# A hybrid decoder layer on one core: row maxima 0.75 of a head ahead of the attention instead of 0.65, and the maxima given during a wait for a shift counted

## The chip, the core and the metric

The kernel runs on one core of one Trainium2 chip. The metric is device time in microseconds (us) of one execution, lower is better. The core has a matrix engine (TensorE, called PE), a vector engine (DVE), a scalar engine (ACT), a general engine (POOL), and a queue engine (SP) that issues most transfers; each runs its own list of instructions in order and waits on the others through semaphores.

## What is computed

One layer of a decoder: a prompt of 2048 positions with model width 1024, and eight sampled positions with a paged cache (the sampled part is not touched by the change). RMSNorm and one input projection give q, k, v of 8 heads of 64, a forget gate, and the features za, u, gv, zc. One half is attention with a forget term, the other a spatial gating inside chunks of 128; both are gated and go through one output projection.

```python
def fox_prompt(q, k, v, logf):            # c is the running sum of logf
    ...
        s = jnp.einsum('bqhd,bkhd->bhqk', qb, kf) * SCALE
        s = s + cb[:, :, :, None] - c[:, :, None, :]
        s = jnp.where(pos_k[None, :] <= pos_q[:, None], s, -jnp.inf)
        pr = jax.nn.softmax(s, axis=-1)
        return jnp.einsum('bhqk,bkhd->bqhd', pr, vf)
...
def merge(x, attn, za, mix, u, zc, w_out):
    a = attn.astype(x.dtype).reshape(B, S, D_ATT) * jax.nn.silu(za)
    m = (u * mix.astype(x.dtype)).reshape(B, S, D_CHK) * jax.nn.silu(zc)
    return x + jnp.concatenate([a, m], axis=-1) @ w_out
```

## The kernel before

PE's program order is written out by hand; the other engines' instructions are issued by the same code as it goes along, and each engine runs them in that order. A clock in the code (`Pe.clock`, a sum of nominal costs of what has been put on PE) says when loads and late pieces of work are issued. The program has three stretches: the input products (to about 585 us), the attention loop (585 to about 1140 us), and the output products.

**The attention loop** goes over 32 units (head h, block c of 512 queries) in the order of the list `UNITS`. A unit has 4c+4 key tiles of 128 keys. For each key tile `values` puts on PE a pair of matmuls into a PSUM bank `sc` (three banks), on diagonal tiles with a small mask matmul between them; ACT takes the exponential into a tile `p` (line 1059, ten slots in turn); POOL adds `p` into the denominator `acc` (lines 1066 and 1068), and PE multiplies the `p` tiles with the values in batches of eight (`av`).

**The maxima.** Softmax needs a shift per query. It is the row maximum of the scores, computed ahead by a generator, `all_maxima` (its object is `mgen`), that runs head by head: matmuls of up to 512 columns into three PSUM banks `tp` (in the trace `tp<-k,q`), each followed by a DVE reduction of the bank (`mn<-tp`, lines 993 and 995). When four query tiles, one block c, are done, `shifts` has the result transposed on PE, copied by ACT (`rows<-tp`, line 1014) and stored by SP (`mrow<-rows`, line 1017), and puts (h, c) in the set `shifted`. A head has 17408 columns of maxima and the whole attention 8 heads of them. The first maximum of head h needs the head's key tile `k`, whose last three rows come from `kx` by a transfer on SP's queue (line 909). `load_head(h + 1)` queues these loads when unit (h, 0) reaches its second key tile, and they are issued one at a time as `Pe.clock` goes on.

**The rate of the maxima.** `mdone[0]` is the work of maxima given so far, `vdone` that of the key tiles; `MT` and `VT` are one head's share of each. In front of the first unit maxima are given until `mdone[0]` reaches `AHEAD * MT`. After each key tile the loop gives maxima as long as

```python
            while mdone[0] / MT < min(vdone / VT + AHEAD, NH):
```

**Waiting for a shift.** Four key tiles before a unit's end (or earlier) `values` calls `load_queries` for the next unit, which issues four transfers on SP's queue (lines 953 to 955; the last is the shift, from `mrow`). If the unit's shift isn't in `shifted`, `load_queries` takes maxima from the generator until it is (or calls `give`, which takes other filling products, when no maxima are left).

**Filling products** between key tiles are feature products (`fl<-hh,fh` and the like, three matmuls of 512 columns each time) and at the end output products.

**The end of the loop.** `load_out_weights` loads eight blocks of the output weights (`raw`, three buffers, line 1137); each is cast on ACT (`wo<-raw`, line 268) and subtracted on DVE (line 273) in the same queues that hold the exponentials and the reductions. `out_inputs` loads two tiles of 512 KB, `g` and `xy`, for each output row tile (lines 1171 and 1172), and casts `g` on ACT into `am`.

Of the kernel before, what the change touches and what calls it, by code (L numbers as in the profile page):

```python
# [56 lines left out]
NTP = 3  # L57
NAV = 1
UNITS = [(h, c) for h in range(6) for c in range(4)] + [(6, 0), (6, 1), (6, 2), (7, 0), (6, 3), (7, 1), (7, 2), (7, 3)]
AHEAD = 0.65  # L60
LSTEP = 3000.0
LHEAD = 2500.0
VPARTS = 7
# [23 lines left out]
def hymba_step(ctx, tc, x_prompt, x_sample, cache_k, cache_v, cache_logf, page_table, g_norm, w_in,  # L87
# [84 lines left out]
    def give():  # L172

        seen, last = len(nc.cur_bb.bb.instructions), Pe.last
        Pe.waiting.pop(0)[2]()
        for i in nc.cur_bb.bb.instructions[seen:] if last is not None else ():
            if i.engine != mybir.EngineType.PE:
                tc.add_manual_dep(i, last.name, mybir.DependencyInfo(mybir.DependencyClass.NoSync,
                                                                     mybir.DependencyReason.DATA), reason="given late")

    def pump(all_=False):
        while Pe.waiting and (all_ or Pe.waiting[0][0] <= Pe.clock):
            give()
        if not all_ and Pe.loads and Pe.clock >= Pe.load_at:
            load_next()
        if not all_ and Pe.clock >= Pe.side:
            m = next(mgen)
            mdone[0] += m
            Pe.side = Pe.clock + PACE if mdone[0] < AHEAD * MT else 1e12
        if not all_ and Pe.clock >= Pe.decode:  # L190
            Pe.decode = Pe.clock + (next(Pe.steps, None) or 1e12)

    def load_next():
        Pe.loads.pop(0)()
        Pe.load_at = Pe.clock + LSTEP
# [738 lines left out]
    def place(t):  # L934

        at = places.setdefault(t, [])
        if len(at) < 2:
            at.append(s4(F32R, t))
            nc.gpsimd.memset(at[-1][HD:HD + 3, 512 if t == "q2" else 0:].bitcast(F32), 1.0)
        else:  # L940
            at.append(at.pop(0))
        return at[-1]

    def load_queries(h, c):
        while (h, c) not in shifted:
            if next(mgen, None) is None:
                give()
            pump()

        t = place("q2")  # L950
        a, cs = h * HD, slice(c * 512, (c + 1) * 512)
        for r in range(2):
            nc.sync.dma_start(t[r * HD:(r + 1) * HD, :512].bitcast(F32), qk_hi[a:a + HD, cs])
        nc.sync.dma_start(t[:HD, 512:].bitcast(F32), qk_lo[a:a + HD, cs])
        nc.sync.dma_start(t[HD + 2:HD + 3, 512:].bitcast(F32), mrow[h:h + 1, cs])
        return t
# [79 lines left out]
    def values(at):  # L1036
# [3 lines left out]
        for kt in range(4 * c + 4):  # L1040
# [3 lines left out]
            if at + 1 < len(UNITS) and UNITS[at + 1] not in qload and kt >= 4 * c + 4 - (  # L1044
                    QLEAD if UNITS[at + 1] in shifted else 4):
                qload[UNITS[at + 1]] = load_queries(*UNITS[at + 1])
# [69 lines left out]
    def all_maxima():  # L1116
        for h in range(NH):
            while h not in heads or "k2" not in heads[h] or h and len(Pe.loads) > VPARTS:
                if not Pe.loads:
                    raise RuntimeError(h)  # L1120
                load_next()
            yield from maxima(heads[h])
# [109 lines left out]
    mgen = all_maxima()  # L1232
    mdone = [0.0]
# [113 lines left out]
    Pe.side = 1e12  # L1347
    while mdone[0] < AHEAD * MT:
        c = next(mgen)
        mdone[0] += c  # L1350
        fill(c * PRE)
        pump()
        if UNITS[0] in shifted and UNITS[0] not in qload:
            qload[UNITS[0]] = load_queries(*UNITS[0])
    if UNITS[0] not in qload:
        qload[UNITS[0]] = load_queries(*UNITS[0])
    vdone = 0.0
    for at, (h, c) in enumerate(UNITS):
# [5 lines left out]
        for v in values(at):  # L1364
            vdone += v
            fill(v * dose)
            pump()
            while mdone[0] / MT < min(vdone / VT + AHEAD, NH):
                m = next(mgen, None)
# [49 lines left out]
```

## Time and profile before

| what | value |
|---|---|
| runs | 1324.32, 1329.95, 1331.84 us; median 1329.95 us |
| profiled execution | 1327.27 us, of it 1325.5 us from its first to its last instruction (the span) |
| PE busy in the span | 1294.4 us (98%) |
| DVE, ACT, POOL busy | 49%, 33%, 42% |
| mean granted clock of PE | 0.990 of full speed |

All stretches that follow are in us from the span's start, in this one profiled execution. "Busy" of PE counts a matmul at half clock as longer, so a busy PE may still be a slow one. Start to start is the better measure of a matmul, as neighbours overlap.

### The profile page before, as it was taken

What the parts mean: (1) busy time and instruction counts of PE and PEld (TensorE: products, weight loads), DVE (VectorE), ACT (ScalarE), POOL (GpSimd) and SP (SyncE); (2) the same over time, 40 slices, a digit from 0 to 9 for tenths busy, and PEclk for the clock granted to TensorE, in tenths of its full rate; (3) what the DMA queues carried; (4) which work ended last, traced back from release to release, by engine and by line L of the source; (5) the groups of instructions that cost most, each with busy time, mean ns of one, the idle gap of its engine ahead of it and who ended that gap; (6) DMA issues with size and microseconds to landing.
All of it is one profiled execution on the core that took longest, in us unless ns stands there. A gap on an engine that the chain in (4) does not pass through costs nothing.

```text
span 1325.5 us, 19295 instructions
## 1 busy us (share of the span) xinstructions
PE 1294.4 (98%) x6544; PEld 1005.0 (76%) x6544; DVE 653.7 (49%) x1217; ACT 432.0 (33%) x781; POOL 559.9 (42%) x587
## 2 busy tenths in 40 slices
PE   6999999999999999999999999999999998999998
PEld 6999999999887877866666666666666564688877
DVE  5446664534678654254476544454455544422321
ACT  5542322222222111124444544344444356200100
POOL 3113343423232456215667565567567468600000
PEclk9999999999999999999999999999999898999999
DMA  7644353555213878946344856766474445573221
GB/s 218 197 122 106 88 144 112 151 144 149 73 43 83 291 240 261 310 112 157 81 129 132 221 137 164 205 175 174 131 204 118 112 131 173 184 265 118 96 81 48
DMA packets 189172, 201.43 MB, mean 152 GB/s; under 512 B 40018, under 2 KB 138642, under 8 KB 189050
## 3 DMA queue, kind: packets, MB, share of 16 engines
q1 hardware_dynamic: 185186, 191.43, 50.4%
q10 hardware_dynamic: 3488, 8.39, 1.7%
q8 instruction: 52, 0.85, 0.3%
q14 instruction: 46, 0.38, 0.1%
q0 software_dynamic: 400, 0.38, 0.1%
HBM read 127.43 MB, written 72.73 MB: 151 GB/s over the span
## 4 chain that ended last, share of the span: by engine, by line
PE 89%; DVE 3%; DMA 3%; issue 2%; ACT 1%; POOL 1%; SPq 1%; POOLq 0%; DVEq 0%; ACTq 0%
PE acc L198 35%; PE sc L198 23%; PE fl L198 10%; PE av L198 9%; PE tp L198 6%; PE tp L202 4%; PE pm L198 3%; POOL acc L1068 1%; DMA raw<-in_w_out_dram 1%; DVE mn L995 1%; DMA xp<-in_x_prompt_dram 0%; DMA wraw<-in_w_in_dram 0%; DVE mn L993 0%; DVE wl L281 0%; ACT p L1059 0%
## 5 line engine op out<-in xcount | busy, mean ns | idle before, releaser
L1068 POOL TENSOR_TENSOR acc<-acc,p 128x512 f32<-128x512 f32 (+3 forms) x256 | 289.4, 1131 | 78.7 <-ACT p L1059 63.1
L1059 ACT ACTIVATE p<-sc,zero 128x512 f32<-128x512 f32 (+1 forms) x320 | 194.0, 625 | 171.0 <-PE sc L198 162.6
L198 PE MATMUL acc<-wh,hh 128*128 128x384 f32 (+2 forms) x640 | 228.7, 357 | 0.8 <-ACT hh L268 0.8
L198 PE MATMUL acc<-wl,hh 128*128 128x384 f32 (+2 forms) x640 | 222.5, 348 | 1.0 <-DVE wl L281 1.0
L198 PE MATMUL acc<-wh,hl 128*128 128x384 f32 (+2 forms) x640 | 222.8, 348 | 0.7 <-DVE hl L273 0.6
L198 PE MATMUL sc<-q,k 128*128 128x512 f32 (+7 forms) x640 | 202.7, 398 | 6.7 <-ACT p L1059 6.6
L198 PE MATMUL sc<-wo,am 128*128 128x512 f32 x720 | 164.1, 390 | 0.0
L198 PEld LDWEIGHTS sc<-wo,am 128*128 128x128 f32 x720 | 134.9, 188 | 28.2
L995 DVE TENSOR_REDUCE mn<-tp 128x1 f32<-128x320 f32 (+5 forms) x192 | 118.9, 632 | 75.5 <-PE tp L198 74.6
L198 PEld LDWEIGHTS sc<-q,k 128*128 128x128 f32 (+1 forms) x640 | 119.1, 197 | 27.1 <-ACT p L1059 11.4
L198 PE MATMUL av<-p,vst 128*64 128x512 f32 (+3 forms) x640 | 137.2, 549 | 0.0
L198 PE MATMUL tp<-k,q 66*128 66x384 f32 (+6 forms) x320 | 122.3, 399 | 8.5 <-DMA k<-kx 1.7
L198 PEld LDWEIGHTS acc<-wh,hh 128*128 128x128 f32 x640 | 120.7, 189 | 8.2 <-ACT hh L268 1.5
L198 PEld LDWEIGHTS acc<-wh,hl 128*128 128x128 f32 x640 | 120.4, 188 | 6.8 <-DVE hl L273 1.6
L198 PEld LDWEIGHTS acc<-wl,hh 128*128 128x128 f32 x640 | 120.8, 189 | 5.9 <-DVE wl L281 1.4
L261 POOL TENSOR_SCALAR sm<-sm 128x6 f32<-128x6 f32 (+3 forms) x84 | 20.3, 242 | 243.4 <-DVE sm L447 169.9
L198 PEld LDWEIGHTS av<-p,vst 128*64 128x64 f32 x640 | 48.8, 139 | 68.2 <-issue 58.6
L993 DVE TENSOR_REDUCE mn<-tp 128x1 f32<-128x512 f32 (+7 forms) x128 | 66.8, 563 | 53.2 <-PE tp L198 52.7
L262 POOL TENSOR_TENSOR sm<-sm,mhalf 128x6 f32<-128x6 f32 (+3 forms) x84 | 89.0, 1060 | 6.7
L198 PEld LDWEIGHTS tp<-k,q 66*128 66x128 f32 x320 | 60.6, 191 | 37.6 <-DVE mn L995 6.2
L1066 POOL TENSOR_TENSOR acc<-p 128x512 f32<-128x512 f32 x32 | 41.1, 1284 | 110.4 <-ACT p L1059 98.9
L1194 DVE TENSOR_TENSOR xy<-xy,sc 128x512 f32<-128x512 f32 x30 | 20.6, 687 | 120.1 <-PE sc L198 120.1
(213 smaller groups left out, 1902.3 us busy)
## 6 DMA issues: line engine op xcount, KB each, us to landing
kb<-in_cache_k_dram SPq DMA_DIRECT2D x32, 256.0 KB
k<-qk_hi SPq DMA_DIRECT2D x32, 256.0 KB
q<-qk_hi SPq DMA_DIRECT2D x64, 128.0 KB
vb<-in_cache_v_dram SPq DMA_DIRECT2D x32, 256.0 KB
g<-gm SPq DMA_DIRECT2D x16, 512.0 KB
xy<-in_x_prompt_dram SPq DMA_DIRECT2D x16, 512.0 KB
out_dram<-xy ACTq DMA_DIRECT2D x15, 512.0 KB
qk_hi<-qkh SPq DMA_DIRECT2D x32, 192.0 KB
```

The costliest lines, as they stand in the source:

```text
L198: Pe.last = nc.tensor.matmul(out, lhsT, rhs, start=start, stop=stop).ins
L202: Pe.last = nc.tensor.transpose(out, in_, idn).ins
L261: nc.gpsimd.tensor_scalar(r, ss, inv_n, EPS, op0=ALU.mult, op1=ALU.add)
L262: nc.gpsimd.tensor_tensor(r, r, mhalf[:rows, :n], op=ALU.pow)
L993: nc.vector.tensor_reduce(part[:, j_ % 4, n_:n_ + 1], sp, axis=AX.X, op=ALU.min)
L995: nc.vector.tensor_reduce(part[:, j % 4, n:n + 1], sp, axis=AX.X, op=ALU.min)
L1059: nc.scalar.activation(p[:, n0:], sp[:, n0:], AF.Exp, bias=zero1, scale=-1.0)
L1066: nc.gpsimd.tensor_tensor(acc, p0, p, op=ALU.add)
L1068: nc.gpsimd.tensor_tensor(acc[:, n0:], acc[:, n0:], p[:, n0:], op=ALU.add)
L1194: nc.vector.tensor_tensor(xy[:, fs], xy[:, fs], po, op=ALU.add)
```

## The change

The constant `AHEAD` goes from 0.65 to 0.75, and in `load_queries` the maxima that are given while a shift is awaited are added to `mdone[0]`, as the main loop does for its own. Before, those maxima were given without being counted, so the main loop went on giving its share as if they were still to come.

```diff
@@ -57,7 +57,7 @@
-AHEAD = 0.65
+AHEAD = 0.75
@@ -943,8 +943,11 @@
     def load_queries(h, c):
         while (h, c) not in shifted:
-            if next(mgen, None) is None:
+            m = next(mgen, None)
+            if m is None:
                 give()
+            else:
+                mdone[0] += m
             pump()
```

Lines behind the second place are three higher in the changed kernel (line 1059 is 1062 there). The set of instructions is the same on every engine; PE's order is the same for the input products and, names aside, from the last third of unit (7, 1) on.

The first place is on PE near the end of unit (6, 2), where the unit (7, 0) is next and its shift is awaited. `k` and `q` behind `tp<-` are the key and query tiles of head 7; `tp<-ident` are small transposes, `identb` and `maskb` the mask. Before:

```order
L202 MATMUL tp_10876<-ident,mn_10715 4x128
L198 MATMUL tp_10884<-k_1897_10642,q_999_6032 128x384
L202 MATMUL tp_10887<-ident,sm_10859 4x128
L198 MATMUL tp_10890<-k_1897_10642,q_999_6032 128x384
L198 MATMUL tp_10893<-k_1897_10642,q_999_6032 128x384
L198 MATMUL tp_10895<-k_1897_10642,q_999_6032 128x256
L198 LDWEIGHTS identb
L198 MATMUL tp_10893<-maskb,identb 128x128
L198 LDWEIGHTS identb
L198 MATMUL tp_10895<-maskb,identb 128x128
L198 MATMUL tp_10901<-k_1897_10642,q_999_6032 128x512
L198 MATMUL tp_10904<-k_1897_10642,q_999_6032 128x512
```

And now, behind the same batch of `av`:

```order
L202 MATMUL tp_10903<-ident,mx_10841 4x128
L198 MATMUL tp_10907<-k_1900_10653,q_999_6032 128x512
L202 MATMUL tp_10910<-ident,sm_10886 4x128
L198 MATMUL sc_10913<-q_1030_6174,k_1784_10064 128x512
L198 LDWEIGHTS identb
L198 MATMUL sc_10913<-maskb,identb 128x128
L198 MATMUL sc_10913<-q_1030_6174,k_1765_9971 128x512
L198 MATMUL tp_10919<-k_1900_10653,q_999_6032 128x512
L198 MATMUL sc_10922<-q_1030_6174,k_1784_10064 128x384
L198 LDWEIGHTS identb
L198 MATMUL sc_10922<-maskb,identb 128x128
L198 MATMUL sc_10922<-q_1030_6174,k_1765_9971 128x384
```

Before, this is the start of 17 maxima with no key tile between them (the piece goes on for another nine maxima); now one maximum stands between two key tiles, and the others have moved to key tiles of (6, 2) and of the units behind it. The longest row of maxima without a key tile or a filling product between them is three now.

The second place is on PE in unit (6, 1), where the first maxima of head 7 stand (`k_1897` before, `k_1900` now, is head 7's key tile; `k_1756` and `k_1765` are head 6's). Before:

```order
L198 MATMUL sc_10688<-q_1047_6244,k_1756_9937 128x512
L198 MATMUL tp_10693<-k_1756_9937,q_999_6032 128x512
L198 MATMUL sc_10697<-q_1047_6244,k_1786_10080 128x512
L198 LDWEIGHTS identb
L198 MATMUL sc_10697<-maskb,identb 128x128
L198 MATMUL sc_10697<-q_1047_6244,k_1756_9937 128x512
L198 MATMUL tp_10703<-k_1756_9937,q_999_6032 128x512
L198 MATMUL sc_10706<-q_1047_6244,k_1786_10080 128x384
L198 LDWEIGHTS identb
L198 MATMUL sc_10706<-maskb,identb 128x128
L198 MATMUL sc_10706<-q_1047_6244,k_1756_9937 128x384
L198 MATMUL tp_10716<-k_1897_10642,q_988_5997 128x128
```

And now:

```order
L198 MATMUL fl_10569<-hh_636,fl_10234 128x512
L198 MATMUL sc_10659<-q_1051_6262,k_1784_10064 128x512
L198 MATMUL sc_10659<-q_1051_6262,k_1765_9971 128x512
L202 MATMUL tp_10662<-ident,acc_6162 128x128 x4
L198 MATMUL tp_10677<-k_1765_9971,q_999_6032 128x512
L198 MATMUL sc_10680<-q_1051_6262,k_1784_10064 128x512
L198 MATMUL sc_10680<-q_1051_6262,k_1765_9971 128x512
L198 MATMUL tp_10685<-k_1765_9971,q_999_6032 128x512
L198 MATMUL sc_10688<-q_1051_6262,k_1784_10064 128x512
L198 MATMUL sc_10688<-q_1051_6262,k_1765_9971 128x512
L198 MATMUL tp_10699<-k_1900_10653,q_988_5997 128x128
L198 MATMUL tp_10701<-k_1900_10653,q_988_5997 128x256
```

The first maximum of head 7 stood behind the unit's sixth key tile, and stands behind its third. The first maxima of the other heads move by about as much: head 3's stood behind the second key tile of a unit, and stand behind the first diagonal tile of the unit in front of it.

The third place is SP's queue near the end of the loop. `q` are the queries of the last unit, (7, 3), `mrow<-rows` is the store of its shift. Before:

```order
L953 DMA q_1047_6244<-qk_hi 64x512 x2
L954 DMA q_1047_6244<-qk_lo 64x512
L955 DMA q_1047_6244<-mrow 1x512
L1082 DMA aT<-at_11372 64x512
L1161 DMA gm<-ga_11268 128x4x128
L1171 DMA g_11425<-gm 128x1024
L1172 DMA xy_11426<-in_x_prompt_dram 128x1024
L1171 DMA g_11429<-gm 128x1024
L1172 DMA xy_11430<-in_x_prompt_dram 128x1024
L1137 DMA raw_11388<-in_w_out_dram 128x512
```

And now:

```order
L1175 DMA xy_11421<-in_x_prompt_dram 128x1024
L1174 DMA g_11424<-gm 128x1024
L1175 DMA xy_11425<-in_x_prompt_dram 128x1024
L1020 DMA mrow<-rows 4x128
L956 DMA q_1051_6262<-qk_hi 64x512
L1140 DMA raw_11390<-in_w_out_dram 128x512
L1140 DMA raw_11406<-in_w_out_dram 128x512
L956 DMA q_1051_6262<-qk_hi 64x512
L1140 DMA raw_11439<-in_w_out_dram 128x512
L957 DMA q_1051_6262<-qk_lo 64x512
L1102 DMA rT<-rows 4x128
L958 DMA q_1051_6262<-mrow 1x512
```

The four query loads of the last unit stood in front of the `g` and `xy` loads; now they stand behind them and between four of the weight loads, since the last shift is stored later (its transpose on PE stands 78 rows later).

## Rows read from the trace of the kernel before

**Rows 1.** The page's busy time (share of the span, instructions) and PE's row of granted clock, a digit for each 33 us (9 is 90% or more).

```profile
PE 1294.4 (98%) x6544; PEld 1005.0 (76%) x6544; DVE 653.7 (49%) x1217; ACT 432.0 (33%) x781; POOL 559.9 (42%) x587
...
PEclk9999999999999999999999999999999898999999
```

**Rows 2.** Waits of PE from 700 us on: what it waited for, us in total, times, longest.

```profile
PE sc L198 <- ACT p L1059: 6.6, 3, 3.4
PE tp L198 <- DMA k<-kx: 1.7, 1, 1.7
```

**Rows 3.** Stretches: us, busy time of PE, PEld, DVE, ACT and POOL with instructions, PE's granted clock (1.00 is 2.4 GHz, 0.50 is 1.2 GHz), DMA share, GB/s.

```profile
560.00:1000.00 440.00, 434.98 (x2190) 284.96 (x2189) 228.07 (x409) 189.26 (x340) 258.15 (x235) 1.00 0.58 156
1047.20:1057.50 10.30, 9.78 (x30) 5.85 (x30) 5.75 (x12) 2.36 (x5) 3.44 (x4) 0.50 0.24 68
1084.80:1088.20 3.40, 3.40 (x11) 2.27 (x10) 0.00 (x0) 1.89 (x4) 3.17 (x4) 0.50 0.70 215
1118.90:1129.20 10.30, 8.82 (x21) 3.63 (x22) 9.00 (x6) 8.16 (x14) 9.79 (x7) 0.50 0.61 206
```

**Rows 4.** Timeline of PE around the 17 maxima: start, us from the first start to the last end, instruction, count, and in brackets the idle time before it.

```profile
1041.14 0.42 PE L198 MATMUL tp<-k,q 66*128 66x384 f32 x1
...
1046.05 3.63 PE L198 MATMUL tp<-k,q 66*128 66x512 f32 x6
...
1050.87 0.78 PE L198 MATMUL sc<-q,k 128*128 128x512 f32 x1
...
1055.20 2.61 PE L198 MATMUL av<-p,vst 128*64 128x512 f32 x8
```

**Rows 5.** Timeline of DVE, then ACT, then POOL in the same stretch.

```profile
1043.52 2.48 DVE L995 TENSOR_REDUCE mn<-tp 128x1 f32<-128x512 f32 x4
...
1052.41 0.69 ACT L1059 ACTIVATE p<-sc,zero 128x512 f32<-128x512 f32 x1 [10.45 <-PE sc L198]
...
1053.24 3.15 POOL L1068 TENSOR_TENSOR acc<-acc,p 128x512 f32<-128x512 f32 x3 [9.65 <-ACT p L1059]
```

**Rows 6.** Timeline of PE, then POOL, then SP's queue at the first maxima of head 7 (the key tile's rows come by `k<-kx`).

```profile
1019.84 0.39 PE L198 MATMUL tp<-k,q 66*128 66x512 f32 x1
...
1020.54 0.40 PE L198 MATMUL tp<-k,q 66*128 66x512 f32 x1
1020.77 0.40 PE L198 MATMUL sc<-q,k 128*128 128x512 f32 x1
...
1023.97 0.47 PE L198 MATMUL tp<-k,q 66*128 66x128 f32 x2 [1.71 <-DMA k<-kx]
...
1019.07 1.28 POOL L571 TENSOR_TENSOR mxu<-mxu,sz 128x512 f32<-128x512 f32 x1 [2.35 <-DVE sz L548]
...
1020.38 0.38 SPq L572 DMA_DIRECT2D gm<-mxu  x1
1020.80 0.37 SPq L909 DMA_DIRECT2D k<-kx  x1
```

**Rows 7.** Timeline of PE, then SP's queue, at the first maxima of head 3 (the two matmuls of 128 and 256 columns at 750.93).

```profile
743.78 0.39 PE L198 MATMUL tp<-k,q 66*128 66x512 f32 x1
...
750.93 0.40 PE L198 MATMUL tp<-k,q 66*128 66x128 f32 x2
...
741.98 0.46 SPq L909 DMA_DIRECT2D k<-kx  x1
```

**Rows 8.** Timeline of PE, then ACT, in unit (6, 3).

```profile
1083.73 0.73 PE L198 MATMUL sc<-q,k 128*128 128x512 f32 x2 [1.68 <-ACT p L1059]
...
1078.62 0.62 ACT L268 CAST wo<-raw 128x512 fp32r<-128x512 f32 x1 [2.73 <-DMA raw<-in_w_out_dram]
...
1081.78 0.62 ACT L268 CAST wo<-raw 128x512 fp32r<-128x512 f32 x1 [1.17 <-DMA raw<-in_w_out_dram]
```

**Rows 9.** Timeline of PE, then ACT, then SP's queue, then POOL around the start of unit (7, 3).

```profile
1112.12 1.50 PE L198 MATMUL av<-p,vst 128*64 128x512 f32 x8
1113.56 1.68 PE L198 MATMUL sc<-q,k 128*128 128x512 f32 x6
1118.65 1.02 PE L198 MATMUL sc<-q,k 128*128 128x512 f32 x2 [3.42 <-ACT p L1059]
...
1122.22 3.30 PE L198 MATMUL sc<-q,k 128*128 128x512 f32 x6 [1.48 <-ACT p L1059]
...
1117.27 0.62 ACT L268 CAST wo<-raw 128x512 fp32r<-128x512 f32 x1 [2.98 <-DMA raw<-in_w_out_dram]
...
1119.58 2.00 ACT L268 CAST am<-g 128x1024 fp32r<-128x1024 f32 x2
...
1099.26 1.09 SPq L953 DMA_DIRECT2D q<-qk_hi  x2
...
1106.96 0.33 SPq L1171 DMA_DIRECT2D g<-gm  x1
...
1109.46 1.91 SPq L1137 DMA_DIRECT2D raw<-in_w_out_dram  x2
...
1115.04 6.40 SPq L1137 DMA_DIRECT2D raw<-in_w_out_dram  x3
...
1105.89 11.58 POOL L1068 TENSOR_TENSOR acc<-acc,p 128x256 f32<-128x256 f32 x9
1119.26 1.28 POOL L1066 TENSOR_TENSOR acc<-p 128x512 f32<-128x512 f32 x1 [1.78 <-ACT p L1059]
```

## The prediction, made before the changed kernel was run

> **What bounds the kernel now.** I began with the page's busy times: PE is busy 98% of the span, and its granted clock is below full only in three of the forty slices, all near the end [rows 1]. So time can only be won or lost in two ways: PE stands still, or PE runs at half clock. PE's waits from 700 us on come next. There are few of them: three waits for an exponential, 6.6 us together, and one of 1.7 us for the rows of head 7's key tile [rows 2]. The windows then show where the clock fell: granted 1.00 from 560 to 1000, and 0.50 in stretches of 10.3, 3.4 and 10.3 us that begin at 1047.2, 1084.8 and 1118.9 [rows 3]. The timelines tell what went before each fall. Before the first, PE gave 17 maxima in a row from 1041.14 to 1050.87 [rows 4], and DVE reduced them one after the other at 2.48 / 4 = 0.62 us each [rows 5], while PE alone needs 0.23 us for one of 512 columns (from 1020.54 to 1020.77) [rows 6]. With only three `tp` banks, DVE set the pace. This doesn't show as idle time, because the trace spreads it over long matmuls (six in 3.63 us) [rows 4]. ACT had no exponential to do for 10.45 us and POOL nothing to add for 9.65 [rows 5]. Before the second fall PE waited 1.68 us for ACT, which waited 2.73 and 1.17 us for weight loads that stand in its queue in front of exponentials [rows 8]. Before the third it waited 3.42 us, again with ACT behind a weight load, and 1.48 us more inside the slow stretch [rows 9].
>
> **The change part by part.** No instruction is added; all terms come from moved ones.
>
> *The row of 17 maxima goes.* It took 1050.87 - 1041.14 = 9.73 us. The same matmuls at full clock and PE's own pace are at most 17 x 0.23 = 3.9 us, and I allow 0.7 for the masks and transposes among them, an estimate. Spread between key tiles, each reduction of 0.62 us has a pair of score matmuls or more beside it, so DVE no longer paces them. Gain 9.73 - 4.6 = 5.1 us; it would be less only if the new places were crowded too, and the longest row is three now, as many as there are banks.
>
> *The half clock after it goes.* From 1050.87 to 1057.5 PE had key tiles and values to do and did them at half speed (eight `av` in 2.61 us there [rows 4], in 1.50 at full clock [rows 9]). Half of 6.6 us is 3.3 us. It goes if the fall came of the row of maxima, as the order of the rows says; otherwise nothing.
>
> *The stall in unit (6, 3).* It cost 1.68 us and half of the 3.4 us at half clock after it, 3.4 us together [rows 3, 8]. Part of the maxima now stands in this unit and gives PE other work while ACT waits for the weights. ACT's clump of casts is still there. Between nothing and 3.4 us I take 2.0.
>
> *Head 7's first maxima come three key tiles earlier.* The rows `k<-kx` are issued at 1020.80, right behind `gm<-mxu` on SP's queue, which waits for POOL's product, started at 1019.07 when DVE's `sz` was done; PE got them at 1023.97 after 1.71 us [rows 6]. The feature product that leads to `sz` stands where it stood, so the rows come no earlier. PE now wants them behind the third key tile, where a maximum of head 6 started at 1019.84 [rows 6]. The wait becomes 1023.97 - 1019.84 = 4.1 us, 2.4 more. Everything on PE is queued behind it, and ACT and POOL run dry.
>
> *The other heads.* Head 3's rows were issued at 741.98 and first used at 750.93; they are now wanted at about 743.78 [rows 7]. With the 3.2 us that head 7's took from issue to use [rows 6] they are there at 745.2, a wait of 1.4 us, unless the issue moves ahead too. Heads 4 to 6 may see less or the same: between 0 and 4 us in all, and I take 0.7, since the load is issued by a clock that runs with PE's order.
>
> *The clock behind head 7's wait.* PE stood 1.71 us there and the clock stayed [rows 3, 6]. The wait of 3.42 us was followed by 10.3 us at half clock, with 1.48 of it idle anyway, so (10.3 - 1.5) / 2 = 4.4 us lost; the wait of 1.68 us by 3.4 us, 1.7 lost [rows 3, 8, 9]. A wait of 4.1 us is nearest to the longest of these, so I expect a fall, and between 1.7 and 4.4 I take 3.0. No fall is the other bound, 0.
>
> *The last unit's queries.* They were issued from 1099.26, more than 14 us before the unit's first matmuls at 1113.56 [rows 9]. Now the low half and the shift stand behind two `g` and `xy` pairs and behind three more weight loads, the third of which needs a buffer that the weight load in front of all this gives back. The nearest row for such a load is 1109.46 to its cast at 1117.27, 7.8 us behind 2 MB of `g` and `xy` [rows 9]. Issued with the first `g` at 1107, cast and subtracted in 1.2 (an estimate, from the cast of 0.62), then three issues at some 0.5 and 3.2 us to use: 1107 + 7.8 + 1.2 + 1.5 + 3.2 = 1120.7, which would be a wait of 7.1 us where 3.42 + 1.48 = 4.9 stand now. That is 2.2 more. It is less, down to 0, if the load in front no longer queues behind the 2 MB; a gain of up to 4.9 would need the stall to vanish altogether. I take +1.5. The half clock there stays.
>
> *In front of the first unit* five more maxima run at DVE's pace: at most 5 x (0.62 - 0.23) = 2 us, and with feature products between them I take 0.7.
>
> **Sum.** -5.1 - 3.3 - 2.0 + 2.4 + 0.7 + 3.0 + 1.5 + 0.7 = -2.1 us on the profiled 1327.27, so 1325.2. The median of the runs is 2.7 us above that execution, which makes 1327.9; I predict 1328 for the median.
>
> **The rivals.** What a measurement of this kernel tells from no change is about 0.5%, 6.6 us.
>
> (a) The forecast, a large gain mostly given back at head 7: -6 to +2 us, 1324 to 1332. Chance 0.38.
>
> (b) The gain is kept. The clock holds behind head 7's wait as it did behind 1.71 us, head 3 doesn't wait, and the last unit's stall shrinks by 2: -5.1 - 3.3 - 3.4 + 2.4 - 2 = -11.4, so 1318.5. For it speaks that the falls followed stretches in which PE had been thin for longer than one wait [rows 4, 9]; against it the length of the wait. Chance 0.28.
>
> (c) Slower: the last unit's queries. If the weight load in front of them lands late and the following loads share the transfers with 2 MB, the chain above runs with its 7.8 us twice, 7.8 more than the +1.5 counted. That gives -2.1 + 7.8 = +5.7, and with another 2 to 4 us at half clock behind the longer wait +8 to +10, so 1338. It decides from a wait of some 14 us in unit (7, 3). For it speaks that three waits (a buffer, `rT`, the shift) now lie in one queue; against it that POOL and ACT come earlier as well. Chance 0.17.
>
> (d) The change moves nothing: POOL, which adds without a pause from 1105.89 to 1117.5 and again from 1119.26 [rows 9], is the real end of the last units, and what PE wins earlier it waits for there. Against it: POOL loses an idle 9.65 us by the change itself [rows 5]. 1330. Chance 0.10.
>
> (e) The maxima that now stand at DVE's pace in front of the first unit pull the clock down there: another 3 us as above, 1331. Against it: the clock is 1.00 in the whole stretch from 560 to 1000, in which maxima also cycle through the three banks [rows 3]. Chance 0.07. The Trainium skill ("TensorE: Matmul & The Clock Gate", section "A second HAM failure mode: psum-queue depth-cycling") says that a matrix engine that cycles through PSUM banks and idles briefly between groups can make the clock go to and fro. By that rule the spread maxima would be no better than the row of 17, and the first two terms would be gone; the trace disagrees so far, with 1.00 over 440 us of such cycling.
>
> **How the numbers follow.** Faster by over 0.5%: (b) and the best edge of (a), 0.33. Slower: (c), 0.17. Within: 0.50. The range goes from the good end of (b), with the head 7 wait shorter by another 2.4, to the bad end of (c): 1316 to 1339. For (a) alone it is 1324 to 1332.
>
> **What would show it.** Right: no row of more than three `tp<-k,q` on PE near 1040; granted clock 1.00 there; a wait of `tp` for `k<-kx` of about 4 us near 1020, followed by a stretch at 0.50; a wait of 5 to 8 us at the start of unit (7, 3), now for `q` or behind casts. Wrong: a fall of the clock where the row of maxima was; waits for `k<-kx` at several heads; or no wait for the rows at all, if SP's queue issues them earlier.

## The result and the profile after

The changed kernel takes 1332.88 us (median of 20 runs), the kernel before 1329.55 us (median of 20). The ratio is 1.0029 with a 95% interval of 1.0017 to 1.0040: slower by 0.3%, within the half per cent that the prediction called no change, but in the other direction than its 1328. The profiled execution takes 1331.16 us, its span 1329.2 us, 3.7 us more than the span of before.

The row of 17 maxima is gone, and so is the half clock behind it. But the page shows a new weak slice for PE's clock [rows 1], a little past the middle, at some 745 us, and the slice around 1045, in which the row's half clock lay, has gone from 8 to 7.

```profile
PE 1294.2 (97%) x6544; PEld 1009.5 (76%) x6544; DVE 646.3 (49%) x1217; ACT 431.7 (32%) x781; POOL 558.9 (42%) x587
...
PEclk9999999999999999999999899999999799999999
```

PE's waits from 700 us on (what it waited for, us in total, times, longest) answer to [rows 2]. The wait for the rows of a key tile has grown from 1.7 to 6.0 us, three times now, and a wait for queries is new:

```profile
PE tp L198 <- DMA k<-kx: 6.0, 3, 4.0
PE sc L198 <- DMA q<-qk_hi: 4.5, 1, 4.5
PE sc L198 <- ACT p L1062: 1.9, 2, 1.8
PE tp L198 <- ACT rows L1017: 1.9, 5, 0.7
PE tp L198 <- DVE mn L996: 1.6, 2, 1.0
```

The windows (us, busy times of PE, PEld, DVE, ACT, POOL, granted clock, DMA share, GB/s) show three stretches at half clock, as [rows 3] did, at other places: behind the first maxima of head 3, behind those of head 7, and around the start of unit (7, 3).

```profile
747.90:754.80 6.90, 6.90 (x24) 3.29 (x23) 1.75 (x3) 1.42 (x3) 3.12 (x4) 0.51 0.91 229
755.00:1031.00 276.00, 268.56 (x1365) 173.37 (x1361) 131.17 (x236) 122.07 (x219) 171.66 (x155) 1.00 0.60 162
1031.10:1044.80 13.70, 13.53 (x46) 8.31 (x47) 5.22 (x10) 3.05 (x6) 6.23 (x6) 0.50 0.34 75
1123.30:1130.20 6.90, 6.29 (x15) 4.46 (x16) 3.83 (x4) 6.40 (x11) 4.23 (x4) 0.51 0.23 69
```

At head 3, PE and then SP's queue, against [rows 7]: PE waits 1.31 us, and 16 `av` then take 5.65 us at half clock. The rows are issued at 744.08, behind four query loads, where they were issued at 741.98.

```profile
744.98 0.40 PE L198 MATMUL fl<-hh,fl 128*128 128x512 f32 x1
746.68 0.47 PE L198 MATMUL tp<-k,q 66*128 66x128 f32 x2 [1.31 <-DMA k<-kx]
...
749.78 5.65 PE L198 MATMUL av<-p,vst 128*64 128x512 f32 x16
...
740.43 1.08 SPq L956 DMA_DIRECT2D q<-qk_hi  x2
...
743.23 0.24 SPq L958 DMA_DIRECT2D q<-mrow  x1
...
744.08 0.46 SPq L909 DMA_DIRECT2D k<-kx  x1
```

At head 7, the same, against [rows 6]:

```profile
1026.61 0.64 PE L198 MATMUL sc<-q,k 128*128 128x512 f32 x2
1031.27 0.77 PE L198 MATMUL tp<-k,q 66*128 66x128 f32 x2 [4.02 <-DMA k<-kx]
...
1039.62 5.80 PE L198 MATMUL av<-p,vst 128*64 128x512 f32 x16
...
1027.80 0.38 SPq L572 DMA_DIRECT2D gm<-mxu  x1
1028.23 0.37 SPq L909 DMA_DIRECT2D k<-kx  x1
```

**Where the time went.** The start of each unit's first score matmul in the two timelines, after minus before. The third column takes off what PE had already done more of by then (maxima and feature products, 0.23 us for each matmul of 512 columns), so that it holds lost time alone.

| point | after - before | lost |
|---|---|---|
| unit (0, 0) | 591.21 - 589.28 = 1.9 | 0.4 |
| unit (2, 1) | 737.69 - 733.91 = 3.8 | 0.2 |
| unit (2, 2) | 756.63 - 749.68 = 7.0 | 5.5 |
| unit (6, 1) | 1024.77 - 1017.38 = 7.4 | 6.7 |
| unit (6, 2) | 1046.71 - 1029.04 = 17.7 | 16.8 |
| unit (7, 0) | 1060.99 - 1058.06 = 2.9 | 5.4 |
| unit (7, 1) | 1096.71 - 1092.17 = 4.5 | 3.4 |
| unit (7, 2) | 1105.21 - 1101.41 = 3.8 | 3.8 |
| unit (7, 3) | 1123.68 - 1113.56 = 10.1 | 10.1 |
| end of the span | 1329.2 - 1325.5 = 3.7 | 3.7 |

So head 3 costs 5.3 us (in unit (2, 1)), head 7 costs 10.1 us (in unit (6, 1)), the going of the row of maxima gives 11.4 back, unit (6, 3) 2.0 more, and the last units come out even. That was read from one execution each; the experiments, and a second profile of each kernel, say which of it belongs to the kernel.

### The profile page after: what moved, and what is told of

Read it like the earlier page. It is cut to its first block, busy times and chain, and to the rows that moved or that the text cites. A ratio compares the mean times of both kernels' runs of the same rounds, so it can differ in the third digit from the quotient of the medians.

```text
span 1329.2 us, 19315 instructions
## 1 busy us (share of the span) xinstructions
PE 1294.2 (97%) x6544; PEld 1009.5 (76%) x6544; DVE 646.3 (49%) x1217; ACT 431.7 (32%) x781; POOL 558.9 (42%) x587
```

## The experiments

Theory 1: the earlier maxima ask for the rows `k<-kx` before SP's queue has brought them; PE stands still, and the clock falls behind the wait. Theory 2: the clock falls there for another reason, and the wait is only beside it. All ratios are against the kernel before, with their 95% intervals; a place's time in a profile is the difference of the starts of two units, as in the table.

**The rows together with the first half of the key tile**, in the changed kernel.

```diff
-        return [lambda: keys(0), rows_of, lambda: keys(1)], [
+        return [lambda: (keys(0), rows_of()), lambda: keys(1)], [
```

> The changed kernel, with the rows of a head's key tile (`k<-kx`) issued together with the first half of the key tile instead of one load step later. Theory 1 (the rows come late on SP's queue, PE waits, and the clock falls behind the wait): at head 3 the rows land before 746, at head 7 they are issued near 1021.4 and are there by 1024.6, before PE wants them at 1027.2. The waits of 1.31 and 4.02 us go, and with them the half-clock stretches from 747.9 and from 1031.1, worth 3.4 and 6.9 us: 1.3 + 4.0 + 3.4 + 6.9 = 15.6 us less, perhaps 3 to 5 of it given back in the last units: 1317 to 1322 us. Theory 2 (the clock falls because the maxima now stand closer to DVE's pace there, with or without a wait): only the waits go, 5 us, and the half-clock stretches stay: about 1328.

Measured: 1319.08 us, ratio 0.9913 (0.9894 to 0.9931), 13.8 us less than the changed kernel and inside theory 1's range. Against the first profile of before, head 3 now costs 1.2 us instead of 5.3 and head 7 0.6 instead of 10.1. PE's waits from 700 to 1080 us have no `k<-kx` any more, the rows of head 7 are issued at 1018.81, nine us earlier than in the changed kernel, and the whole stretch runs at full clock:

```profile
PE tp L198 <- ACT rows L1017: 1.9, 5, 0.7
...
PE tp L198 <- DMA k<-qk_hi: 0.5, 1, 0.5
...
1018.25 0.51 SPq L906 DMA_DIRECT2D k<-qk_hi  x1
1018.81 0.51 SPq L909 DMA_DIRECT2D k<-kx  x1
...
700.00:1060.00 360.00, 353.89 (x1812) 230.26 (x1812) 184.62 (x332) 164.48 (x299) 231.80 (x211) 1.00 0.60 165
```

**The same edit in the kernel before.**

```diff
-        return [lambda: keys(0), rows_of, lambda: keys(1)], [
+        return [lambda: (keys(0), rows_of()), lambda: keys(1)], [
```

> The kernel before with the same edit of the loads (rows of the key tile together with its first half). There only head 7 waited, 1.71 us, and no fall of the clock came behind it. Both theories: 1.7 us less, about 1328, the row of 17 maxima and the half clock behind it as before. If the earlier rows are worth 10 us or more here too, it isn't the waits that the change made that they repair.

Measured: 1325.82 us, ratio 0.9971 (0.9956 to 0.9985): 3.7 us less, not 1.7, and far from 13.8. The two microseconds more fit the second profile of before, below, in which the clock falls behind head 7's wait: from unit (6, 1) to (6, 2) this version takes 10.0 us, where the two profiles of before take 11.7 and 14.6. The mean granted clock of its eleven runs is 0.9895, that of the 28 runs of before beside them 0.9876; times 1328 us that is 2.5 us, an estimate.

**PE kept busy through the waits**, in the changed kernel: matmuls without use in front of the first maximum.

```diff
+DUMMY = {3: 5, 7: 17}
...
+                        if (i, j, n) == (0, 0, 0):
+                            for _ in range(DUMMY.get(h, 0)):
+                                k1 = heads[h - 1]["k1"]
+                                nc.tensor.matmul(sp, k1[:, :P], k1[:, :512], start=True, stop=True)
```

> The changed kernel with matmuls of no use in front of the first maximum of head 3 (5 of 512 columns) and of head 7 (17), so that PE is busy while it would wait for the rows; their results are overwritten. Theory 1 with standing still as the cause of the fall: the time of the waits stays as it is, but the clock doesn't fall behind them: 3.4 + 6.9 = 10.3 us less than the changed kernel, about 1323. Theory 2: the falls stay, and the time is that of the changed kernel, 1333, or a little more.

Measured: 1326.76 us, ratio 0.9964 (0.9948 to 0.9980), 6.1 us less than the changed kernel, with more work and the rows as late as they were. At head 7 the rows are issued at 1030.58, 3.5 us behind the start of unit (6, 1), as in the changed kernel; the 17 matmuls stand where PE stood still, and the clock holds from 740 to 1110:

```profile
1028.94 0.64 PE L199 MATMUL sc<-q,k 128*128 128x512 f32 x2
1029.42 4.16 PE L992 MATMUL tp<-k 128*128 128x512 f32 x17
1033.62 0.46 PE L199 MATMUL tp<-k,q 66*128 66x128 f32 x2
...
1030.58 0.37 SPq L910 DMA_DIRECT2D k<-kx  x1
...
713.10:720.00 6.90, 6.78 (x17) 2.34 (x19) 5.58 (x11) 1.69 (x4) 5.10 (x4) 0.51 0.61 190
740.00:1110.00 370.00, 363.92 (x1840) 234.13 (x1840) 185.57 (x325) 171.59 (x310) 236.96 (x214) 1.00 0.59 163
```

In the profile, from unit (6, 1) to (6, 2) this takes 6.1 us less than in the changed kernel, and from (2, 1) to (2, 2) 2.7 us less, 8.8 of the 10.3 expected. So the fall comes of standing still, and theory 2 is out for these two places. The rest went elsewhere in this execution: 3.4 us in a stretch at half clock at 713.1, behind a wait of 0.99 us for DVE that the changed kernel has too, without a fall in its profiles, and 1.9 us in front of the first unit, where the two programs are the same.

**Head 7's rows alone early**, in the changed kernel.

```diff
-        return [lambda: keys(0), rows_of, lambda: keys(1)], [
+        return [lambda: (keys(0), rows_of()), lambda: keys(1)] if h == 7 else [lambda: keys(0), rows_of, lambda: keys(1)], [
```

> The changed kernel, with the rows of head 7's key tile alone issued together with the tile's first half; head 3 as in the changed kernel. Theory 1 (wait and fall at each place for themselves): head 7's wait of 4.02 us and the 6.9 us of half clock behind it go, head 3's stay: 10.9 us less than the changed kernel's 1332.9, about 1322, and 3 us above the version with the early rows at all heads (1319.1). If head 3's loss is not of its own but one event somewhere in a stretch (the rival), the time is that of the version with early rows everywhere, 1319.

Measured: 1326.26 us, ratio 0.9968 (0.9957 to 0.9980), 6.6 us less than the changed kernel and 7.2 more than with early rows at all heads. So head 7's place and the other heads' have prices of their own, but nearer to each other than 10.9 and 3. In the profile (6, 1) to (6, 2) takes 9.3 us less than in the changed kernel; 2.8 us of that are lost in front of the first unit, where the programs are the same, and 0.9 at head 3, which waits 2.20 us here and loses its clock. The stretch of head 7 is at full clock:

```profile
750.37 0.47 PE L198 MATMUL tp<-k,q 66*128 66x128 f32 x2 [2.20 <-DMA k<-kx]
...
750.80:757.80 7.00, 7.00 (x26) 3.67 (x25) 2.37 (x5) 1.42 (x3) 3.04 (x4) 0.51 0.85 237
1024.00:1050.00 26.00, 24.84 (x134) 15.87 (x135) 15.81 (x32) 14.38 (x26) 19.14 (x19) 1.00 0.69 191
```

**The changed kernel once more**, for a second profile.

> The changed kernel once more, for a second profile. If the falls of the clock at head 3 and head 7 belong to the kernel, both stretches at 0.50 are there again, near 748 and 1031, each behind the wait for `k<-kx`; if a fall is a matter of the single execution, one or the other is missing or stands elsewhere.

Measured: 1333.8 us. Both falls are there: half clock from 749.8 to 756.7 behind a wait of 2.07 us, and from 1033.1 to 1046.8 behind one of 4.12 us.

```profile
748.83 0.47 PE L198 MATMUL tp<-k,q 66*128 66x128 f32 x2 [2.07 <-DMA k<-kx]
...
1033.43 0.77 PE L198 MATMUL tp<-k,q 66*128 66x128 f32 x2 [4.12 <-DMA k<-kx]
...
749.80:756.70 6.90, 6.90 (x23) 3.37 (x24) 1.99 (x4) 1.42 (x3) 2.64 (x4) 0.51 0.92 236
1033.10:1046.80 13.70, 13.37 (x46) 8.31 (x47) 5.21 (x10) 3.05 (x6) 6.21 (x6) 0.50 0.34 75
```

**The kernel before once more.**

> The kernel before once more, for a second profile. The half clock behind the row of 17 maxima (1047 to 1057) is there again if it belongs to the row; PE waits some 1.7 us for the rows of head 7, with the clock at 1.00 behind it as in the first profile, or with a fall, if it is a matter of the single execution.

Measured: 1327.19 us. The row of 17 has its half clock again, from 1047.1 to 1060.8. And behind head 7's wait, 1.59 us here, the clock falls this time, for 6.9 us:

```profile
1023.40 0.76 PE L198 MATMUL tp<-k,q 66*128 66x128 f32 x2 [1.59 <-DMA k<-kx]
...
1023.20:1030.10 6.90, 6.70 (x24) 3.99 (x26) 2.13 (x5) 1.09 (x3) 5.58 (x6) 0.51 0.49 110
1047.10:1060.80 13.70, 13.13 (x37) 7.18 (x36) 8.29 (x16) 2.35 (x5) 3.44 (x4) 0.50 0.28 89
...
1086.58 0.74 PE L198 MATMUL sc<-q,k 128*128 128x512 f32 x2 [1.47 <-ACT p L1059]
...
1083.00:1110.00 27.00, 25.53 (x122) 14.79 (x122) 7.42 (x11) 17.77 (x33) 21.42 (x20) 1.00 0.44 129
```

So the 1.71 us without a fall of the first profile [rows 3, 6] was one outcome of two. The other way round, PE waits 1.47 us in unit (6, 3) here without the fall that stood behind 1.68 us in the first profile [rows 8].

With the two second profiles the places come out as follows (lost time, in brackets from the first two): head 3 6.1 us (5.3), head 7 7.1 (10.1), the row of maxima -12.0 (-11.4), unit (6, 3) -0.2 (-2.0), from unit (7, 2) to the end 1.9 (-0.1).

**Counting alone**, 0.65 ahead.

```diff
-            if next(mgen, None) is None:
+            m = next(mgen, None)
+            if m is None:
                 give()
+            else:
+                mdone[0] += m
```

> The kernel before with the second part of the change alone (maxima given during a wait are counted, 0.65 ahead). The row of 17 maxima stands where it stood, since counting comes after giving; only the places behind it move. All theories: the time of before, 1329.5 within 2 us, so that what the change does is done by 0.75. A time of 1333 would put the loss on the counting.

Measured: 1333.35 us, ratio 1.0020 (1.0005 to 1.0035): 1.9 us above the range that was expected. The row of 17 stands; the maxima behind it are given later, the last shift with them, and the last unit's queries fall behind the `g` and `xy` loads as they do in the changed kernel. PE waits 6.25 us for them:

```profile
1119.79 3.75 PE L198 MATMUL sc<-q,k 128*128 128x512 f32 x8 [6.25 <-DMA q<-qk_hi]
```

From unit (7, 2) to the end its profile has 227.3 us where before has 224.1, so the loss lies in good part there. The counted line isn't what makes the changed kernel slower, though: with 0.75 ahead no unit ever waits for its shift while maxima are left, so the counted line is never reached, and the order of instructions on all five engines is row for row that of 0.75 alone. The change as measured is the change of the constant.

**Queries in front of the wait**, on top of early rows: the three loads of the next unit's queries go out ten key tiles before a unit's end, and the shift's when it is there.

```diff
+            if at + 1 < len(UNITS) and kt >= 4 * c + 4 - QLEAD and UNITS[at + 1] not in qload \
+                    and UNITS[at + 1] not in shifted and UNITS[at + 1] not in qpre:
+                qpre[UNITS[at + 1]] = load_parts(*UNITS[at + 1])
```

> The changed kernel with early rows at all heads, and the queries of the next unit (three of the four loads) issued ten key tiles before a unit's end even where the shift isn't there yet; for the last unit they now stand in front of the `g` and `xy` loads. If the queries behind 2 MB are what the last unit waits for (5.5 us there), 3 to 5 us less than 1319.1, about 1315. If the shift, which is still stored late and read behind a weight load and `rT`, or ACT's casts set the end of the wait, the wait only changes its name: 1318 to 1320.

Measured: 1318.38 us, ratio 0.9917 (0.9902 to 0.9931), 0.7 us less than without it, well inside the intervals. In the profile unit (7, 3) starts 5.3 us earlier, and the end is where it was. The wait has changed its name, to the shift and then to ACT:

```profile
1107.47 0.50 PE L198 MATMUL sc<-q,k 128*128 128x512 f32 x1
1109.60 1.45 PE L198 MATMUL sc<-q,k 67*128 67x512 f32 x5 [1.62 <-DMA q<-mrow]
1112.81 1.22 PE L198 MATMUL sc<-q,k 128*128 128x512 f32 x2 [1.76 <-ACT p L1072]
```

**One pair of `g` and `xy` in front of the last unit instead of two**, on top of that.

```diff
-OFIRST = 2
+OFIRST = 0
```

> The version with early rows and early queries, and one pair of `g` and `xy` (1 MB) instead of two loaded in front of the last unit. The stretch from the start of unit (7, 2) to the end has had 224 to 225 us in five versions, whether PE waited for the queries in it or for ACT. If ACT's casts of weights, which land behind the 2 MB, hold it at that, the casts come 2 to 4 us earlier and the stretch is 220 to 222 us, the time 1314 to 1317. If something else holds it (POOL's adds, the half clock there), the stretch stays at 224 to 225 and the time at 1318.

Measured: 1316.03 us, ratio 0.9893 (0.9857 to 0.9930). From the start of (7, 2) to the end the profile has 1317.2 - 1096.0 = 221.2 us, where it had 224.1 before, 224.0 after, 225.0 with early rows and 224.9 with early queries. The time is in the range that was expected if ACT's casts hold the stretch, but this doesn't show that they do. PE runs at half clock for 10.3 us of the stretch with early queries and for 3.4 us here, and half of that difference, some 3.4 us, is nearly all of the 3.7:

```profile
1111.40:1121.70 10.30, 8.89 (x21) 4.41 (x23) 6.62 (x5) 7.10 (x12) 8.91 (x7) 0.50 0.60 206
...
1117.20:1120.60 3.40, 3.40 (x9) 0.99 (x10) 2.60 (x2) 1.69 (x4) 3.40 (x4) 0.50 1.03 329
```

Whether the one pair shortened the half clock, or the single execution did, isn't shown; the intervals of the two versions overlap. (The profile of this version also has a fall at 748.6, behind a wait of 1.60 us of head 3 for a key half.)

**0.85 of a head ahead**, with early rows at all heads.

```diff
-AHEAD = 0.75
+AHEAD = 0.85
```

> The changed kernel with early rows at all heads and 0.85 of a head ahead. The last shift is stored before the `g` and `xy` loads and the last unit's four loads stand in front of them. Theory: the wait for the queries in the last unit (5.5 us) goes, ACT's casts keep 2 to 3 us of it; in turn the first maxima of each head come another 3 key tiles earlier, so that even the early rows are late at one head or another, by up to 3 us with a fall of the clock behind it: between 1314 (no row late) and 1325 (a fall at two heads). Near 1319 if both come out even.

Measured: 1325.21 us, ratio 0.9968 (0.9956 to 0.9979), the upper end. The early rows are late again at head 3, by 5.95 us where at most 3 were expected, and at head 7 by 0.80; with head 3's wait the clock is at half from 748.9 to 755.7:

```profile
750.44 0.76 PE L198 MATMUL tp<-k,q 66*128 66x128 f32 x2 [5.95 <-DMA k<-kx]
```

**0.70 of a head ahead**, with early rows at all heads.

```diff
-AHEAD = 0.75
+AHEAD = 0.70
```

> The changed kernel with early rows at all heads and 0.70 of a head ahead, which is enough for the row of maxima to go (the longest has three) and asks for the rows some two key tiles later than 0.75. Theory: no wait for the rows, no fall of the clock at heads 3 and 7, no row of 17: the time of the version with 0.75 and early rows, 1319, or 1 us less for the heads' small waits. If it is at 1325 or above, 0.75 itself, and not only the absence of the row, is worth something.

Measured: 1316.61 us, ratio 0.9903 (0.9867 to 0.9940). No wait for a key tile's rows and no fall between 585 and 1085. It is 2.5 us less than with 0.75, though the intervals overlap. In the profile the gain lies in the last units: 221.6 us from (7, 2) to the end, with 3.4 us at half clock there instead of 6.8 (from 1111.3) with 0.75, and with two pairs of `g` and `xy` still in front of the last unit's queries.

**The two best edits together**: 0.70, early rows, one pair of `g` and `xy`.

```diff
-AHEAD = 0.75
+AHEAD = 0.70
...
-OFIRST = 2
+OFIRST = 0
```

> The two best edits together: early rows at all heads with 0.70 of a head ahead, and one pair of `g` and `xy` in front of the last unit instead of two. If both gains are of their own (no waits for rows; weights that land earlier), 2 us less than with 0.70 alone, about 1314.5. If 0.70 had already taken the stall in the last units (its stretch from (7, 2) to the end was 221.6 us, as short as that with one pair), the time stays at 1316.6 within 1 us.

Measured: 1312.40 us, ratio 0.9869 (0.9838 to 0.9901), the fastest of all, 1.3% below the kernel before. It is 2 us below the sum of the two gains, which its interval doesn't tell from the sum. The granted clock is full from the first unit to 1300, and PE's waits in the last units are down to 2.5 us:

```profile
585.00:1300.00 715.00, 705.72 (x3446) 482.72 (x3447) 335.08 (x554) 271.95 (x481) 363.37 (x321) 1.00 0.52 152
...
PE sc L198 <- ACT p L1062: 1.5, 4, 0.5
PE sc L198 <- DMA q<-qk_lo: 1.0, 1, 1.0
```

## Why the prediction was wrong

The direction was wrong: 2 us less forecast against the median of the runs then shown, 3.3 more measured. Step by step, from the lost time in the table:

- *The row of 17 and the half clock behind it*, forecast -8.4: -11.4. Right in mechanism, too small. All four profiles of versions with the row have that half clock, for 10.3 or 13.7 us, and none of the ten without it; the gain itself varies by execution.
- *The stall in unit (6, 3)*, forecast -2.0: -2.0, with some luck: against the second profile of before, where no fall follows that stall, it is -0.2.
- *Head 7's wait*, forecast 4.1 us, 2.4 more than before: 4.02 and 4.12 us in two profiles. Exact, and for the reason given: the rows still go out right behind `gm<-mxu`.
- *The clock behind head 7's wait*, forecast +3.0 between 1.7 and 4.4: the stretch at half clock is 13.7 us long in both profiles, and nearly all of it was work, so it costs 6.9 us. Against the second profile of before, which loses 3.4 us at this place too, the difference is still 3.4. **This step failed.** I took the bounds from two falls that cost less, and from a part of the longer one being idle. The longest fall then on record was 10.3 us, and nothing bounded a longer one.
- *The other heads*, forecast +0.7: **this step failed too, and it cost the most beyond its forecast.** At head 3 I counted a wait of 1.4 us; it was 1.31 and 2.07 us. The clock got no term there, and no reason was given for that, though a wait of 1.68 us with a fall behind it stood in [rows 3, 8]. The wait of 1.71 us at head 7, behind which the clock had stayed, was no evidence of safety: the second profile of before shows a fall behind 1.59 us at the same place. Half of 6.9 us was lost at head 3, and the whole of it came to 5.3 us. That the wait was close to 1.4 is partly luck: the rows went out behind the next unit's query loads, 2.1 us later than in [rows 7], and PE came to its first maximum 1.6 us later than counted. The other heads together cost 1.3 us.
- *The last unit's queries*, forecast +1.5: -0.1 in the first two profiles, +1.9 in the second two. The wait for the queries came (4.48 us, where I had a stall of 7.1), but the waits for ACT fell from 4.9 us to 1.9, and the stretch at half clock from 10.3 us to 6.9, which together is as much. Rival (c), which priced this at +8, was wrong: its wait of 14 us didn't come. With counting alone, where these loads also stand behind the 2 MB, the stretch took 3.2 us more than in the first profile of before, with a wait of 6.25 us and 13.6 us at half clock. What sets that stretch is open.
- *In front of the first unit*, forecast +0.7: 0.4. Single executions move this by more: unit (0, 0) starts between 591.2 and 594.0 in four profiles of programs that are the same up to there.

The forecast sum of the two failed steps with head 7's wait was 6.1 us; they came to 16.7 (14.3 in the second two profiles). The execution that the forecast was read from was a good one: its mean granted clock is 0.990, that of the 28 runs of before 0.9876, so a part of the 2.7 us that the forecast added for the median is probably falls that this profile doesn't show. Of rival (b), that the clock holds behind the wait, nothing remains. Rivals (d) and (e) showed nowhere: PE's waits don't name POOL (ACT's do, five times for 4.4 us in all), and the clock is at 1.00 where the five more maxima stand in front of the first unit. One reading was off without effect: the page's row of clock shows two slices below 9 and not three [rows 1]; the third fall shows only in [rows 3]. What the experiments showed as cause: the early rows took 13.8 us away where waits and falls, 1.3 + 4.0 + 3.4 + 6.9, make 15.6; and keeping PE busy without ending the waits took 6.1.

What stays open: which of the short waits (about 1 to 2.4 us) is followed by a fall in a given execution. No run here tells.

## What to carry to other kernels

Work that is moved ahead asks earlier for its inputs, so the first question is when each of its loads is issued, and behind what in its queue; here one line that issued a small load earlier turned a loss of 0.3% into a gain of 0.9%. A wait of PE is to be priced with the half clock that may follow it, which at heads 3 and 7, where it came, cost from less than half of the wait to 2.6 times it, and one profile in which nothing followed is not a proof. Where a stretch keeps its length while the name of its wait changes, add up its waits and its half clock before looking for one limit: here a longer wait and a shorter half clock came to the same length.

## What the runs showed of the hardware

The clock's fall behind a short wait is a matter of the execution. The same instructions with a wait of 1.25 us for DVE near 682 kept the clock in both profiles of before, and lost it for 3.4 us in two versions: in that with early rows in the kernel before, from 683.4, and in that with counting alone, which doesn't differ from before up to there, from 684.6. PE's row in the kernel before and in the version with early rows there, then the windows of this version and of counting alone:

```profile
682.13 0.38 PE L198 MATMUL tp<-k,q 66*128 66x256 f32 x1 [1.25 <-DVE sm L1089]
...
682.66 0.38 PE L198 MATMUL tp<-k,q 66*128 66x256 f32 x1 [1.25 <-DVE sm L1089]
...
683.40:686.80 3.40, 3.40 (x11) 2.25 (x12) 2.23 (x7) 0.69 (x1) 1.20 (x1) 0.50 0.25 82
...
684.60:688.00 3.40, 3.37 (x11) 2.36 (x11) 1.48 (x3) 0.94 (x2) 1.28 (x1) 0.50 0.26 82
```

A wait of 0.99 us near 712 was followed by 6.9 us at half clock in the version with the filled waits, by 3.4 us in that with early queries, and by none in the changed kernel. Waits of 2.07 to 5.95 us for a key tile's rows came with a fall each time (five of five), those of 1.3 to 1.7 us two times in four. In the last units three waits for ACT of 2.05, 2.28 and 2.44 us had no fall before PE's next wait. The Trainium skill ("TensorE: Matmul & The Clock Gate", section "A second HAM failure mode: psum-queue depth-cycling") speaks of a matrix engine that cycles through PSUM banks and idles briefly and often between groups of matmuls, which makes the clock go to and fro. The traces agree as to the idles, though here single waits of 1 to 6 us were enough; with PE busy for 268.6 of 276 us the maxima cycled through three banks at a granted clock of 1.00, in the changed kernel's window from 755.
